# Stick-breaking attention: the order of two subtractions in a block, one from PSUM and one of a carry that comes through DRAM

## The chip, the cores and the metric

The kernel runs on one core of a Trainium2 chip. The metric is the device time of one execution in microseconds (us), median of three runs. A profile of one further execution is shown with it. In the profile PE is the matrix engine (PEld its weight load), DVE the vector engine, ACT the scalar engine, POOL GpSimd, and SP the engine that issues most DMAs. L781 is line 781 of the kernel.

## The reference, cut to what matters

One decoder block on 1024 tokens of width 1024: a state-space branch and an attention branch, merged by gates, then a feed-forward part. The change is in the attention branch, which has 8 heads of 64 and works as follows:

```
z        = (q @ k.T) / sqrt(64)                       # one head, 1024 x 1024
mask     = key_pos < query_pos
log_not  = where(mask, log_sigmoid(-z), 0)
suffix   = cumsum(log_not, over keys, reverse) - log_not
weights  = where(mask, exp(log_sigmoid(z) + suffix), 0)
out      = weights @ v
```

So the weight of a key needs the sum of log_not over all later keys up to the query. Since log_sigmoid(z) = z - softplus(z) and log_not = -softplus(z), the exponent is z minus the sum of softplus(z) over this key and all later ones.

## The kernel before, in words

Attention is worked in 40 units, one after the other. There are four pairs of heads (`hp`), each with two halves of 512 queries (`Q`). A half is swept over blocks of 128 keys (`kbs`) from the last to the first, three units for the first half (the last two key blocks share a unit) and seven for the second. So a pair of heads has ten units; I number all of them from 0 to 39, and units 10, 20 and 30 are the first ones of a pair. In every half the first three units lie on the diagonal and need the mask; they have 768, 768 and 1024 columns (two heads together), all others have 1024. Keys are on the partitions, queries on the columns.

What happens to unit i:

- `scores` (L742): PE makes z in PSUM (tile `z`, one buffer). DVE adds the mask (L763), or ACT copies (L765), into `wa`. ACT makes log(1+exp(-|z|)) in three passes (L766 to L768) into `ws`, and DVE makes softplus of it (L769). POOL rounds this to `wh` (L770) and DVE makes the remainder `wl` (L771), so that PE can multiply both parts at its faster rate without losing bits.
- `sums` (L773): PE multiplies a triangle of ones by `wh` and `wl`. The result in PSUM (tile `acc`, one buffer) holds for each key the sum over the keys of this block from it on. What the later blocks sum up to, the carry, comes in `wb` (one buffer), the same row on all 128 partitions. POOL subtracts the carry from `wa` (L781), DVE subtracts `acc` from `wa`, one head at a time (L802), and ACT takes the exponential (L803).
- In the same function the carry for the next unit is made: DVE adds the first row of `acc` to the row so far (L794 or L796, on one partition), SP stores the row into DRAM (L798, tensor `cD`), and SP loads it back on 128 partitions (L800) into `wb`.
- `values` (L805): PE multiplies the weights with V (tile `V`) and sums over the units of a half in PSUM.

The loop `attention` (L815) runs `sums` of unit i, then `values` of unit i-1, then `scores` of unit i+3 (`LOOK = 3`). In between it sets 8 matmuls of other work each time (`fillers`, L703: the projections of q and k for later heads and of a gate; their weights come by L412, are rounded by ACT L419 or POOL L421, and POOL makes the remainder in L422). PE keeps this written order (`pinned`). On DVE, ACT, POOL and SP the order within each engine is set when the program is built, by a scheduler that models when each instruction could start; at run time each engine works its list in that order, and an instruction waits for its operands with all behind it on its engine waiting too. A buffer is given to its next tile when the last reader of the old tile is done. So `acc` of unit i+1 can be written when both L802 of unit i are done, and L800 of unit i can start when L781 of unit i, the last reader of the one `wb`, is done.

The numbers of the buffers touched here are two lines of the program:

```
ZPB, MXB = 1, 2
WAB2, WSB, WHB, RWB, CBB = 5, 2, 2, 2, 1
```

Of the kernel before, what the change touches and what calls it, by code (L numbers as in the profile page):

```python
# [13 lines left out]
ALU = mybir.AluOpType  # L14
# [320 lines left out]
P = 128  # L335
# [57 lines left out]
class Block:  # L393
# [379 lines left out]
    def sums(self, u, work):  # L773


        nc, g, a, f = self.nc, u.group, u.a, u.f
        kb, fs, c = u.segs[-1]
        if g.behind is not None:
            old = slice(c.start + P if kb >= 4 * u.Q else 0, 512)
            o = slice(old.start - c.start, 512 - c.start)  # L780
            nc.gpsimd.tensor_tensor(a[:, :, o], a[:, :, o], g.behind[:, :, old], ALU.subtract)  # L781
        r = self.accp.tile([P, 2, 512], F32, name="acc")
        for x in range(2):
            for n in range(2):
                self.pinned(r[:, x, 0:f], lhsT=self.upto, rhs=u.parts[n][:, x, 0:f], start=n == 0, stop=n == 1 and g.behind is not None)
            if g.behind is None:
                for n in range(2):
                    self.pinned(r[:, x, f - P:f], lhsT=self.ones_r, rhs=u.parts[n][:, x, 0:P], start=False, stop=n == 1)
        if kb:
            past, g.row = g.row, work.tile([P, 2, 512], F32, name="row", bufs=RWB)[0:1]  # L790
            if c.start:
                nc.gpsimd.memset(g.row[:, :, 0:c.start], 0.0)
            if past is None:
                nc.vector.tensor_copy(g.row[:, :, c], r[0:1, :, fs])  # L794
            else:
                nc.vector.tensor_tensor(g.row[:, :, c], past[:, :, c], r[0:1, :, fs], ALU.add)  # L796
            d = self.cD[u.hp, u.Q, kb:kb + 1]
            nc.sync.dma_start(out=d, in_=g.row.rearrange("p a b -> p (a b)"))  # L798
            g.behind = work.tile([P, 2, 512], F32, name="wb", bufs=CBB)
            nc.sync.dma_start(out=g.behind.rearrange("p a b -> p (a b)"), in_=d[0].partition_broadcast(P))  # L800
        for x in range(2):
            nc.vector.tensor_tensor(a[:, x, 0:f], a[:, x, 0:f], r[:, x, 0:f], ALU.subtract)  # L802
        self.last_exp = nc.scalar.activation(a[:, :, 0:f], a[:, :, 0:f], AF.Exp)  # L803

    def values(self, u, out):  # L805
# [605 lines left out]
```

## Time and profile before

| | |
|---|---|
| time, median of 3 runs (lowest to highest) | 1584.97 us (1581.94 to 1589.53) |
| the profiled execution: its own time, its span | 1583.8 us, 1582.1 us |
| busy in the span: PE, DVE, ACT, POOL | 1424.0, 1094.8, 616.2, 821.3 us |
| mean granted clock of PE, as a share of full speed | 0.960 |
| attention: first matmul into `acc`, last exponential done | 420.4 us, 720.6 us from the start of the span |
| L802, DVE, out of PSUM | 80 instructions, 46.8 us busy |
| L781, POOL, the carry | 32 instructions, 67.8 us busy |

Busy is the time in which an engine had an instruction of any kind under way. A row of the profile that groups instructions gives after the bar their busy time, the mean of one, and how long the engine stood idle just before them, with what ended that wait. Idle time of an engine that nobody waits for costs nothing.

### The profile page before, as it was taken

Reading aid. Unit: us, or ns where it says so; the run is one execution under the profiler, and the core shown is the slowest. Engines: PE = TensorE matmul, PEld = TensorE weight load, DVE = VectorE, ACT = ScalarE, POOL = GpSimd, SP = SyncE. Lnnn points to the kernel's source line nnn. Section 1 sums busy time; section 2 is a strip of 40 time slices with the busy share of each in tenths; the row PEclk is TensorE's granted clock in tenths of the full one; section 3 lists DMA queues with packets and bytes.
Section 4 is the critical chain, followed back from the end, with each engine's and each line's share of the span. In section 5 each row is a group of like instructions: output and inputs, shape, how many; then the busy total and the mean of one; then the engine's idle time right before and its main releaser. Section 6 shows DMA issues by size and latency. Waiting matters only on the chain.

```text
span 1582.1 us, 18396 instructions
## 1 busy us (share of the span) xinstructions
PE 1424.0 (90%) x6578; PEld 1117.5 (71%) x6578; DVE 1094.8 (69%) x1317; ACT 616.2 (39%) x792; POOL 821.3 (52%) x642
## 2 busy tenths in 40 slices
PE   4898888799998899989799879999999998999965
PEld 2698767678755555647688668888888887787854
DVE  5548777442577787766723986666665669999978
ACT  5431111452565656565315543233323233433313
POOL 2488684010445454532420636554445468879774
PEclk9899999999999999999899989999999999999988
DMA  8456666635423233236334315333333246545302
GB/s 284 161 142 177 179 188 172 182 106 181 132 80 108 81 97 124 94 101 224 114 142 146 107 40 154 106 113 108 106 100 100 93 164 229 151 142 163 102 22 107
DMA packets 180451, 210.46 MB, mean 133 GB/s; under 512 B 28612, under 2 KB 121896, under 8 KB 180360
## 3 DMA queue, kind: packets, MB, share of 16 engines
q1 hardware_dynamic: 169288, 201.29, 40.1%
q10 hardware_dynamic: 11072, 8.00, 1.8%
q8 instruction: 52, 0.85, 0.2%
q14 instruction: 39, 0.32, 0.1%
HBM read 159.18 MB, written 48.89 MB: 132 GB/s over the span
## 4 chain that ended last, share of the span: by engine, by line
PE 30%; DVE 10%; issue 5%; POOL 4%; ACT 1%; DMA 1%; POOLq 0%; DVEq 0%; ACTq 0%
PE tq L1138 11%; PE wo L1138 9%; PE wo L1019 5%; PE gu L1138 3%; POOL pa L1191 1%; DVE f L1213 1%; POOL wb L1211 1%; POOL pb L1230 1%; DVE pb L1226 1%; DVE x L1226 1%; DVE f L1209 1%; DVE wl L1209 1%; DMA pa<-in_w_ffn_down_dram 1%; DVE ft L438 1%; PE tq L1220 0%
## 5 line engine op out<-in xcount | busy, mean ns | idle before, releaser
L438 POOL TENSOR_TENSOR ws<-wb 128x1024 f32<-128x1024 f32 x29 | 73.2, 2524 | 105.7 <-DVE wl L441 59.9
L770 POOL TENSOR_SCALAR wh<-ws 128x1024 fp32r<-128x1024 f32 (+1 forms) x40 | 38.6, 964 | 124.7 <-DVE ws L769 87.9
L422 POOL TENSOR_TENSOR wl<-ws,wh 128x1024 fp32r<-128x1024 f32 x14 | 37.1, 2656 | 116.3 <-ACT wh L419 106.9
L771 DVE TENSOR_TENSOR wl<-ws,wh 128x1024 fp32r<-128x1024 f32 (+1 forms) x40 | 66.1, 1653 | 36.8 <-POOL wh L770 36.7
L438 POOL TENSOR_TENSOR wgs<-wb 128x1024 f32<-128x1024 f32 x15 | 37.9, 2527 | 101.5 <-DVE x L441 35.1
L781 POOL TENSOR_TENSOR wa<-wa,wb 128x1024 f32<-128x1024 f32 (+2 forms) x32 | 67.8, 2120 | 31.8 <-DMA wb<-cD 26.1
L803 ACT ACTIVATE wa<-wa 128x1024 f32<-128x1024 f32 (+1 forms) x40 | 38.9, 972 | 80.3 <-DVE wa L802 75.8
L802 DVE TENSOR_TENSOR wa<-wa,acc 128x512 f32<-128x512 f32 (+1 forms) x80 | 46.8, 623 | 29.9 <-POOL wa L781 26.7
L871 DVE SCALAR_TENSOR_TENSOR acc<-aw,cond,acc 128x512 f32<-128x512 f32 x56 | 54.7, 978 | 18.1 <-DMA aw<-in_w_ada_dram 17.5
L1191 POOL TENSOR_TENSOR pa<-pa,row 128x1024 f32<-128x1024 f32 x22 | 66.3, 3034 | 1.5 <-DMA pa<-in_w_ffn_down_dram 1.5
L769 DVE SCALAR_TENSOR_TENSOR ws<-wa,ws 128x1024 f32<-128x1024 f32 (+1 forms) x40 | 53.4, 1336 | 16.4 <-ACT ws L768 16.3
L1129 POOL TENSOR_TENSOR f<-f,f 128x512 f32<-128x512 f32 x30 | 49.1, 1661 | 26.0 <-DVE f L1119 17.5
L701 PE MATMUL acc<-wh,upto 128*128 128x512 f32 (+1 forms) x80 | 32.7, 409 | 26.9 <-DVE wa L802 26.2
L766 ACT ACTIVATE ws<-wa 128x1024 f32<-128x1024 f32 (+1 forms) x40 | 38.9, 973 | 37.3 <-DVE wa L763 36.6
L419 ACT CAST wh<-ws 128x1024 fp32r<-128x1024 f32 x28 | 29.2, 1047 | 55.0 <-PE wo L1019 30.2
L1211 POOL TENSOR_TENSOR wb<-pa 128x512 f32<-128x512 f32 x23 | 40.2, 1756 | 15.7 <-DVE wxl L1209 5.5
L1118 ACT ACTIVATE f<-f 128x1024 f32<-128x1024 f32 x22 | 23.3, 1061 | 56.5 <-DVE f L1158 29.1
L701 PE MATMUL z<-q,k 64*128 64x512 f32 (+3 forms) x192 | 41.8, 526 | 3.3 <-DVE wa L763 1.7
L701 PEld LDWEIGHTS acc<-wh,upto 128*128 128x128 f32 x80 | 15.5, 194 | 37.9 <-issue 29.7
L1129 POOL TENSOR_TENSOR f<-f 128x512 f32<-128x512 f32 x20 | 42.2, 2126 | 0.0
L1220 PE MATMUL tq<-f,f 128*128 128x512 f32 x96 | 31.1, 407 | 11.8 <-DVE f L1213 11.8
L1220 PE MATMUL wo<-f,f 128*128 128x512 f32 x132 | 40.7, 389 | 0.0
(818 smaller groups left out, 4888.4 us busy)
## 6 DMA issues: line engine op xcount, KB each, us to landing
aw<-in_w_ada_dram SPq DMA_DIRECT2D x32, 512.0 KB
wb<-cD SPq DMA_DIRECT2D x32, 512.0 KB
hD<-f SPq DMA_DIRECT2D x30, 512.0 KB
ws<-in_w_in_dram SPq DMA_DIRECT2D x23, 512.0 KB
wb<-in_w_ffn_gate_dram SPq DMA_DIRECT2D x44, 256.0 KB
wb<-in_w_ffn_up_dram SPq DMA_DIRECT2D x44, 256.0 KB
pa<-in_w_ffn_down_dram SPq DMA_DIRECT2D x22, 512.0 KB
wb<-hD SPq DMA_DIRECT2D x40, 256.0 KB
```

Source lines behind the costliest of these rows:

```text
L438: (add or nc.gpsimd).tensor_tensor(st, a, b, op)
L701: return self.tc.keep_in_program_order(self.nc.tensor.matmul(*args, **kw))
L769: nc.vector.scalar_tensor_tensor(st, a, 0.0, st, ALU.max, ALU.add)
L771: nc.vector.tensor_tensor(lt, st, ht.bitcast(F32), ALU.subtract)
L781: nc.gpsimd.tensor_tensor(a[:, :, o], a[:, :, o], g.behind[:, :, old], ALU.subtract)
L871: nc.vector.scalar_tensor_tensor(acc, w[:, j], cj, acc, ALU.mult, ALU.add)
L1019: nc.tensor.matmul(ps, lhsT=mg[t // 4][k][:, a, P * (t % 4):P * (t % 4) + P], rhs=ws[k // 2][b][:, k % 2], start=(j == 0), stop=(j == 23))
L1129: nc.gpsimd.tensor_tensor(o, a, b, op)
L1138: self.nc.tensor.matmul(ps, lhsT=w[x][:, q, k], rhs=self.B[i](y, k), start=(j == 0), stop=(j == 11))
L1191: nc.gpsimd.tensor_tensor(w, w, g2, ALU.mult)
L1211: nc.gpsimd.tensor_tensor(st[:, R], u, W[p][b[0]][:, 512 * b[1]:512 * b[1] + 512], SIGN_B[i])
L1220: nc.tensor.matmul(ps, lhsT=o[x][:, P * t:P * t + P], rhs=o[y][:, R], start=(j == 0), stop=(j == 3 * np_ - 1))
```

## The change

POOL's subtraction of the carry moves from the front of `sums` to behind DVE's subtraction out of `acc`. The tile that it reads is kept in a local name, since `g.behind` is by then the tile of the next unit. Nothing else is changed; the number of instructions is the same.

```diff
         nc, g, a, f = self.nc, u.group, u.a, u.f
         kb, fs, c = u.segs[-1]
-        if g.behind is not None:
-            old = slice(c.start + P if kb >= 4 * u.Q else 0, 512)
-            o = slice(old.start - c.start, 512 - c.start)
-            nc.gpsimd.tensor_tensor(a[:, :, o], a[:, :, o], g.behind[:, :, old], ALU.subtract)
+        behind = g.behind
         r = self.accp.tile([P, 2, 512], F32, name="acc")
         for x in range(2):
             for n in range(2):
-                self.pinned(r[:, x, 0:f], lhsT=self.upto, rhs=u.parts[n][:, x, 0:f], start=n == 0, stop=n == 1 and g.behind is not None)
-            if g.behind is None:
+                self.pinned(r[:, x, 0:f], lhsT=self.upto, rhs=u.parts[n][:, x, 0:f], start=n == 0, stop=n == 1 and behind is not None)
+            if behind is None:
...
         for x in range(2):
             nc.vector.tensor_tensor(a[:, x, 0:f], a[:, x, 0:f], r[:, x, 0:f], ALU.subtract)
+        if behind is not None:
+            old = slice(c.start + P if kb >= 4 * u.Q else 0, 512)
+            o = slice(old.start - c.start, 512 - c.start)
+            nc.gpsimd.tensor_tensor(a[:, :, o], a[:, :, o], behind[:, :, old], ALU.subtract)
         self.last_exp = nc.scalar.activation(a[:, :, 0:f], a[:, :, 0:f], AF.Exp)
```

In the kernel after the change the carry's subtraction is L803 (before L781), DVE's subtraction L799 (before L802), the row L793 (before L796), its memsets L789 (before L792), the exponential L804 (before L803). The scheduler sets some neighbours anew. In the rows below a number behind a tile's name is one buffer use: `wa_4366`, `wa_4418`, `wa_4464` and `wa_4518` belong to units 16, 17, 18 and 19, and `wh_4420`, `wh_4466`, `wh_4520`, `wh_4570` and `wh_4618` to units 17 to 21.

POOL between the rounding of unit 17 and that of unit 19, before:

```order
L770 TENSOR_SCALAR wh_4420<-ws_4419 128x1024
L781 TENSOR_TENSOR wa_4366<-wa_4366,wb_4449 128x1024
L422 TENSOR_TENSOR wgl_4485<-wgs_4483,wgh_4484 128x1024
L770 TENSOR_SCALAR wh_4466<-ws_4465 128x1024
L781 TENSOR_TENSOR wa_4418<-wa_4418,wb_4503 128x1024
L770 TENSOR_SCALAR wh_4520<-ws_4519 128x1024
```

The same stretch of POOL after the change:

```order
L770 TENSOR_SCALAR wh_4420<-ws_4419 128x1024
L422 TENSOR_TENSOR wgl_4485<-wgs_4483,wgh_4484 128x1024
L803 TENSOR_TENSOR wa_4366<-wa_4366,wb_4448 128x1024
L770 TENSOR_SCALAR wh_4466<-ws_4465 128x1024
L803 TENSOR_TENSOR wa_4418<-wa_4418,wb_4502 128x1024
L770 TENSOR_SCALAR wh_4520<-ws_4519 128x1024
```

The carry of unit i stands ahead of the rounding of unit i+2 in both; the weight's remainder (L422) changed places with the carry that it followed.

DVE from the subtraction of unit 16 to that of unit 18, before:

```order
L802 TENSOR_TENSOR wa_4366<-wa_4366,acc_4495 128x512 x2
L769 SCALAR_TENSOR_TENSOR ws_4465<-wa_4464,ws_4465 128x1024
L771 TENSOR_TENSOR wl_4467<-ws_4465,wh_4466 128x1024
L796 TENSOR_TENSOR row_4546<-row_4500,acc_4541 1x1024
L802 TENSOR_TENSOR wa_4418<-wa_4418,acc_4541 128x512 x2
L769 SCALAR_TENSOR_TENSOR ws_4519<-wa_4518,ws_4519 128x1024
L763 TENSOR_TENSOR wa_4568<-z_4572,mask_3549 128x2x384
L771 TENSOR_TENSOR wl_4521<-ws_4519,wh_4520 128x1024
L796 TENSOR_TENSOR row_4598<-row_4546,acc_4593 1x1024
L769 SCALAR_TENSOR_TENSOR ws_4569<-wa_4568,ws_4569 128x2x384
L802 TENSOR_TENSOR wa_4464<-wa_4464,acc_4593 128x512 x2
```

The same stretch of DVE after the change:

```order
L799 TENSOR_TENSOR wa_4366<-wa_4366,acc_4494 128x512 x2
L769 SCALAR_TENSOR_TENSOR ws_4465<-wa_4464,ws_4465 128x1024
L771 TENSOR_TENSOR wl_4467<-ws_4465,wh_4466 128x1024
L793 TENSOR_TENSOR row_4545<-row_4499,acc_4540 1x1024
L799 TENSOR_TENSOR wa_4418<-wa_4418,acc_4540 128x512 x2
L769 SCALAR_TENSOR_TENSOR ws_4519<-wa_4518,ws_4519 128x1024
L763 TENSOR_TENSOR wa_4568<-z_4572,mask_3549 128x2x384
L771 TENSOR_TENSOR wl_4521<-ws_4519,wh_4520 128x1024
L793 TENSOR_TENSOR row_4597<-row_4545,acc_4592 1x1024
L799 TENSOR_TENSOR wa_4464<-wa_4464,acc_4592 128x512 x2
```

DVE's order stays, but for one L769 that no longer stands ahead of the subtraction of unit 18.

POOL where a weight with both its steps on POOL (L421 and L422) falls between units 19 and 21, before:

```order
L770 TENSOR_SCALAR wh_4520<-ws_4519 128x1024
L781 TENSOR_TENSOR wa_4464<-wa_4464,wb_4549 128x1024
L792 MEMSET row_4699 1x2x256
L770 TENSOR_SCALAR wh_4570<-ws_4569 128x2x384
L792 MEMSET row_4751 1x2x128
L421 TENSOR_SCALAR wh_4638<-ws_4637 128x1024
L781 TENSOR_TENSOR wa_4518<-wa_4518,wb_4601 128x1024
L422 TENSOR_TENSOR wl_4639<-ws_4637,wh_4638 128x1024
L770 TENSOR_SCALAR wh_4618<-ws_4617 128x2x384
```

The same stretch after the change:

```order
L770 TENSOR_SCALAR wh_4520<-ws_4519 128x1024
L789 MEMSET row_4699 1x2x256
L803 TENSOR_TENSOR wa_4464<-wa_4464,wb_4548 128x1024
L789 MEMSET row_4750 1x2x128
L770 TENSOR_SCALAR wh_4570<-ws_4569 128x2x384
L421 TENSOR_SCALAR wh_4638<-ws_4637 128x1024
L422 TENSOR_TENSOR wl_4639<-ws_4637,wh_4638 128x1024
L803 TENSOR_TENSOR wa_4518<-wa_4518,wb_4600 128x1024
L770 TENSOR_SCALAR wh_4618<-ws_4617 128x2x384
```

Here, too, both steps of the weight now stand ahead of the carry.

## Rows read from the trace of the kernel before

**Rows 1.** Busy us of each engine in stretches: window, length, PE, PEld, DVE, ACT, POOL, PEclk.

```profile
420.00:690.00 270.00, 249.73 (x1109) 158.62 (x1108) 200.06 (x206) 165.38 (x183) 133.48 (x97) 0.99 0.30 99
580.00:620.00 40.00, 40.00 (x181) 25.60 (x179) 29.80 (x32) 26.00 (x29) 21.84 (x16) 1.00 0.30 99
```

**Rows 2.** Who waited for whom: us in total, times, longest, whole span.

```profile
DVE wa L802 <- POOL wa L781: 26.7, 17, 4.6
...
PE acc L701 <- DVE wa L802: 26.2, 19, 5.8
POOL wa L781 <- DMA wb<-cD: 26.1, 17, 3.5
```

**Rows 3.** DVE in time: subtractions of units 0, 8, 15, 18, 35, 38.

```profile
422.26 0.99 DVE L802 TENSOR_TENSOR wa<-wa,acc 128x384 f32<-128x384 f32 x2
...
484.28 1.27 DVE L802 TENSOR_TENSOR wa<-wa,acc 128x512 f32<-128x512 f32 x2
...
537.61 1.27 DVE L802 TENSOR_TENSOR wa<-wa,acc 128x512 f32<-128x512 f32 x2
...
563.10 1.27 DVE L802 TENSOR_TENSOR wa<-wa,acc 128x512 f32<-128x512 f32 x2
...
686.42 1.28 DVE L802 TENSOR_TENSOR wa<-wa,acc 128x512 f32<-128x512 f32 x2 [1.12 <-POOL wa L781]
...
712.27 1.29 DVE L802 TENSOR_TENSOR wa<-wa,acc 128x512 f32<-128x512 f32 x2 [2.96 <-POOL wa L781]
```

**Rows 4.** DVE in time, 538 to 554 us, around units 15 to 17.

```profile
538.80 1.21 DVE L769 SCALAR_TENSOR_TENSOR ws<-wa,ws 128x1024 f32<-128x1024 f32 x1
541.28 1.22 DVE L771 TENSOR_TENSOR wl<-ws,wh 128x1024 fp32r<-128x1024 f32 x1 [1.27 <-POOL wh L770]
...
543.02 1.20 DVE L796 TENSOR_TENSOR row<-row,acc 1x1024 f32<-1x1024 f32 x1
544.96 1.28 DVE L802 TENSOR_TENSOR wa<-wa,acc 128x512 f32<-128x512 f32 x2 [0.74 <-POOL wa L781]
...
549.63 3.40 DVE L771 TENSOR_TENSOR wl<-ws,wh 128x1024 fp32r<-128x1024 f32 x1 [1.27 <-POOL wh L770]
...
554.09 1.27 DVE L802 TENSOR_TENSOR wa<-wa,acc 128x512 f32<-128x512 f32 x2
```

**Rows 5.** POOL in time: start, us, [idle before <-releaser].

```profile
528.07 1.30 POOL L781 TENSOR_TENSOR wa<-wa,wb 128x512 f32<-128x512 f32 x1 [1.88 <-DMA wb<-cD]
...
540.20 1.05 POOL L770 TENSOR_SCALAR wh<-ws 128x1024 fp32r<-128x1024 f32 x1 [4.73 <-PE acc L701]
542.55 2.38 POOL L781 TENSOR_TENSOR wa<-wa,wb 128x1024 f32<-128x1024 f32 x1 [1.30 <-DMA wb<-cD]
...
549.56 2.39 POOL L781 TENSOR_TENSOR wa<-wa,wb 128x1024 f32<-128x1024 f32 x1
...
563.36 0.83 POOL L770 TENSOR_SCALAR wh<-ws 128x768 fp32r<-128x768 f32 x1 [0.55 <-DVE ws L769]
...
568.49 2.38 POOL L422 TENSOR_TENSOR wl<-ws,wh 128x1024 fp32r<-128x1024 f32 x1
```

**Rows 6.** SP in time: the loads of the carry of units 13 and 15.

```profile
522.37 0.33 SPq L800 DMA_DIRECT2D wb<-cD  x1
...
538.98 0.34 SPq L800 DMA_DIRECT2D wb<-cD  x1
```

**Rows 7.** All engines in time, at 640 us: DVE and POOL on unit 30 and 29.

```profile
639.67 0.96 DVE L771 TENSOR_TENSOR wl<-ws,wh 128x768 fp32r<-128x768 f32 x1 [1.47 <-POOL wh L770]
639.90 2.96 POOL L781 TENSOR_TENSOR wa<-wa,wb 128x1024 f32<-128x1024 f32 x1
```

**Rows 8.** PE in time: first matmul into acc of units 20 and 26.

```profile
573.02 0.41 PE L701 MATMUL acc<-wh,upto 128*128 128x384 f32 x1 [1.40 <-DVE wa L802]
...
613.02 0.39 PE L701 MATMUL acc<-wh,upto 128*128 128x512 f32 x1
```

**Rows 9.** ACT in time: the exponential of unit 39.

```profile
719.56 1.06 ACT L803 ACTIVATE wa<-wa 128x1024 f32<-128x1024 f32 x1 [1.61 <-DVE wa L802]
```

## The prediction, made before the changed kernel was run

> **What bounds the kernel now.** I went from the page's busy shares (PE 90% of the span) to the stage that the change touches. The busy time by stretches [rows 1] shows PE busy 249.7 of 270 us from 420 to 690 us, so it stands still for 20 us there, and for some more in the tail up to 720. No more than that could come back. In the 40 us from 580 to 620 it never stands still, so nothing can be won in that part.
>
> The list of waits [rows 2] says why it stands still: 26.2 us, in 19 places, are PE waiting for DVE's subtraction (L802) to give `acc` back. DVE in turn waited 26.7 us in 17 places for POOL's carry (L781), and POOL 26.1 us for the load of the carry. Read quickly, that is one chain, and the change cuts it: `acc` no longer waits for the carry. But the two sums need not be the same events, so I looked at instructions in time.
>
> Two kinds of steps alternate. From unit 15 to unit 16 [rows 3 and 4] DVE subtracts at 537.61, works L769, waits 1.27 us for POOL's rounding, works L771 and the row, waits 0.74 us for the carry and subtracts at 544.96: 7.35 us. From unit 16 to 17 the carry was there early, POOL took it at 549.56 for 2.39 us [rows 5], and DVE's L771, begun 0.07 us later, took 3.40 instead of 1.22 us [rows 4]; the step took 9.13 us. DVE lost 2.2 us without a wait in the list. The reverse is in [rows 7]: a carry that POOL began while DVE was on L771 took 2.96 us instead of 2.38 us, and its end is that of L771 (640.63) plus 2.23.
>
> The Trainium skill ("SBUF — State Buffer", section "SBUF: two separate sides") says that GpSimd and a DVE instruction with two SBUF inputs take a shared port as an exclusive lock, and whoever begins first blocks the other for its whole length. The trace agrees with these two rows. By that rule the carry, wherever it is put, pushes L769 or L771 aside; without it the changed step below would be about 1.2 us shorter, which is my faster rival.
>
> **The change, part by part.** No instruction is added or removed. 32 carries on POOL come to stand behind the subtraction on DVE, and the exponential (ACT) behind the carry.
>
> *Removed: DVE's wait for the carry,* 26.7 us in 17 places. What is late next is DVE's own list. POOL keeps the carry of unit i ahead of the rounding of unit i+2, so the steps line up one behind the other. From one subtraction to the next in the middle of a second half: two L802, 1.20 us until the next begins; L769 1.21; the carry, released while L769 runs and held until its end, 2.38; rounding 1.05 plus 0.05; L771 1.14 until the next begins; row 1.13 [rows 4 and 5]. Sum 8.16 us. The step before the first of these has a carry of 768 columns, three quarters of 2.38, or 1.8: 7.6 us. Steps near the diagonal sum to 5 to 7 us. PE's own pace, from 573.02 to 613.02 in six steps [rows 8], is 6.67 us; these include units of 768 columns, and where most units are full I take 6.9. So PE gets `acc` earlier near the diagonal, and in the middle of each second half it waits for DVE as it does now.
>
> *Moved: the carry and its load.* The load of unit i (L800) may start only when the carry of that unit has been read, since `wb` has one buffer. Now that is one subtraction later. From issue to the carry's start was 3.57 us at unit 16, 5.70 us at unit 14, where a weight's load had been issued 0.9 us before [rows 5 and 6]. In the 8.16 us step the carry ends 4.79 us after the subtraction begins; with 0.1 us for issue the next one may begin 10.57 us after, which leaves 5.67 us for the load. So at both ends of what was seen the load just fits, and I cost it at nothing; its cover is the step itself. If it gets longer, each us is paid in full, because the rounding for unit i+2, then L771 and PE's later `acc`, stand behind the carry on POOL. Behind the load on SP's list are the next row's store, gate stores and weight loads; none is needed within a step.
>
> *Moved with it: the weights' remainder (L422),* now ahead of the carry that it followed. 11 of them fall into attention, 2.38 us each [rows 5]. Beside DVE's row and L802 (2.3 us a step) they are hidden; where L421 stands in front, they are not. From unit 18 to 20, in order: L802 1.20, L769 0.91, carry 2.38, rounding 0.83, L421 1.05 (as a rounding of that size), L771 0.91, L422 2.38, L769 0.91, carry 2.38, rounding 0.83, L771 0.91, row 0.60 = 15.3 us, against 13.3 for two steps at PE's pace. (Units of 768 columns at three quarters; the row of 512 at half of 1.20.) A bound below is zero, all hidden; above, 11 times 2.38 = 26.2 us. I take those places where the list shows a chain, about 7 us in all.
>
> *Moved: the exponential.* It ends about 6 us after the subtraction instead of 2.4. PE wants its values one unit later, a step of 7 to 8 us; PE may be held for a us, which it makes up before the next `acc`. Behind it ACT has three more passes (L766 to L768) of about the exponential's length of 1.06 us [rows 9], and these end about 0.2 us before DVE wants them; where ACT also rounds a weight in between, about a us, DVE waits up to 0.8 us, in four places.
>
> *The sum.* I followed the 40 units with these durations, at each step taking the later of DVE's list and PE's pace, and compare with the subtractions in [rows 3].
> - Units 0 to 8: 60.5 us, before 62.0: -1.5. Most of it at unit 5, where DVE waited for a late load.
> - 8 to 15: 47.8, before 53.3: -5.5. Seven steps, mostly near the diagonal, at PE's 6.7 each are 46.9; before, late carries held DVE at units 9, 11, 12 and 14 (the last is in [rows 5]).
> - 15 to 18: 24.4 (7.6 + 2 x 8.16, and 0.5 for ACT), before 25.5: -1.1.
> - 18 to 35: 128.1, before 123.3: +4.8. Before, PE ran through most of this without waiting. Now 17 steps at 6.9 are 117.3, plus 2.0 at unit 20 (above), 2.2 at unit 24 (the mask addition stands behind L771 behind the carry behind L422, and PE waits for `z`), 4.3 for units 25 to 28 (two steps of 8.16, one of 7.6, a weight), about 2.3 for a mask that comes late at unit 33 and weights before it.
> - 35 to 38: 22.8, before 25.9: -3.1. No wait for the carry.
> - 38 to the end of the last exponential: 12.1, before 8.4 (720.62 less 712.27 [rows 3 and 9]): +3.7. The end is now a chain of carries: 2.5 until POOL may begin the carry of unit 38, 2.4, load 3.65, the last carry 2.4, exponential 1.1.
>
> Together -2.7 us. Behind 720 us PE has work at hand, so the end of attention moves the rest with it. The profiled execution was 1583.8 us, so 1581.1; the median of the runs is 1.2 us above that, so 1582.3.
>
> **The rivals.**
> - *Faster: PE gets `acc` when it wants it.* If the carry slips into DVE's waits for POOL or beside the instructions with a PSUM input, L769 is not in its chain, and a step is 8.16 - 1.2 = 6.95 us, PE's pace. For the 12 long steps (7.97 on average) that is 12.2 us more, and 1570 us; with the places of L422 hidden too, 1563. For it: 26.2 us of PE's waits have just the released buffer as their end. Against it: L771 at 3.40 us, and POOL's order.
> - *Slower: the load with one buffer sets the pace.* Place: 20 carries in the second halves with their load behind the carry before. It decides from 5.67 us from issue to start on, and each us above costs a us a unit: at 6.7 us, 20 us, less the 2.7 won: 1602 us. For it: 5.70 at unit 14 with a weight's 512 KB ahead, and weights now stand directly ahead of more of these loads. Against it: a weight's load needs no carry, so it is issued some us before; in most units 3.6 is what was seen.
> - *Slower: the weights' remainders.* If all 11 stay in the chain (26.2 instead of the 7 counted): 19 us more, 1601 us; half of them, 1592.
>
> **How the numbers follow.** Within 0.5% (7.9 us, about what a measurement of this kernel can tell from no change) is 1577 to 1593. My forecast, waits that trade places, has 0.55 and its own range is 1576 to 1590. The faster rival has 0.25, the load 0.09, the remainders 0.11. Of the forecast a small part lies below 1577, of the remainders' rival a third lies within the bound. That makes 0.28 faster, 0.55 the same, 0.17 slower. The range leaves out a tenth on either side: 1566 to 1597.
>
> **What would show it.** Right: no wait of DVE's L799 (the subtraction) for POOL; PE's wait for `acc` no longer 26 but still 15 to 25 us; L769 or POOL's carry longer by what the other holds; steps of about 8.2 us between full units; at the end two loads in the chain of the last exponential. The forecast is wrong if PE's waits for `acc` fall under 10 us (faster), if POOL's waits for the load grow above 26 us and the rounding stands behind them (the load), or if the units with L421 and L422 take over 10 us a step (remainders).

## The result and the profile after

The changed kernel takes 1577.7 us (median of 11 runs, 1571.1 to 1580.2), the kernel before 1586.8 us beside it. The ratio is 0.9949, 95% interval [0.9935, 0.9963]: 0.5% faster. The forecast was 1582 in a range of 1566 to 1597; the ratio lies at the edge of the 0.5% that the forecast counted as the same. The profiled execution took 1579.3 us, its span 1577.6.

The waits of the changed kernel from 420 to 725 us (us in total, times, longest) answer to [rows 2]:

```profile
ACT wa L804 <- POOL wa L803: 81.3, 31, 5.4
DVE wl L771 <- POOL wh L770: 67.6, 39, 3.3
POOL wa L803 <- DVE wa L799: 49.3, 17, 3.8
...
PE mm L701 <- ACT wa L804: 20.4, 15, 5.3
...
POOL wa L803 <- DMA wb<-cD: 17.3, 6, 4.1
...
PE acc L701 <- DVE wa L799: 7.4, 6, 2.5
```

DVE's 26.7 us of waiting for the carry are gone: L799 never waits for POOL. PE's wait for `acc` fell from 26.2 to 7.4 us, but PE now waits 20.4 us for the exponential, which it did for 0.4 us before. And DVE waits 67.6 us for POOL's rounding, 36.7 before. Waits traded places. The busy time agrees (columns as in [rows 1]):

```profile
420.00:690.00 270.00, 252.80 (x1145) 163.22 (x1142) 195.10 (x214) 169.77 (x190) 148.70 (x98) 1.00 0.31 99
580.00:620.00 40.00, 37.80 (x166) 24.21 (x164) 25.84 (x28) 25.10 (x28) 25.34 (x16) 1.00 0.30 100
```

PE gained only 3 us of work in the first window, and in the second, where it never stood still before, it now does for 2.2 us. The column to look at is POOL's: 148.7 us busy, before 133.5, with one instruction more in the window. Two groups of lines show where these us come from (before, whole span; busy us, mean ns | idle before):

```profile
L781 POOL TENSOR_TENSOR wa<-wa,wb 128x1024 f32<-128x1024 f32 (+2 forms) x32 | 67.8, 2120 | 31.8 <-DMA wb<-cD 26.1 <-ACT ws L768 2.3 <-ACT ws L767 1.6
L771 DVE TENSOR_TENSOR wl<-ws,wh 128x1024 fp32r<-128x1024 f32 (+1 forms) x40 | 66.1, 1653 | 36.8 <-POOL wh L770 36.7
```

The same two after the change:

```profile
L803 POOL TENSOR_TENSOR wa<-wa,wb 128x1024 f32<-128x1024 f32 (+2 forms) x32 | 81.1, 2534 | 72.9 <-DVE wa L799 49.3 <-DMA wb<-cD 17.3 <-ACT gst L738 2.9
...
L771 DVE TENSOR_TENSOR wl<-ws,wh 128x1024 fp32r<-128x1024 f32 (+1 forms) x40 | 52.7, 1317 | 67.7 <-POOL wh L770 67.6
```

The 32 carries take 13.3 us longer, the 40 remainders L771 13.4 us less; L769 takes 53.4 us in both kernels. What DVE and POOL hold each other for was handed from one to the other, not taken away. One step between full units, DVE and POOL in time, answers to [rows 4 and 5]:

```profile
541.11 1.27 DVE L799 TENSOR_TENSOR wa<-wa,acc 128x512 f32<-128x512 f32 x2
542.31 1.21 DVE L769 SCALAR_TENSOR_TENSOR ws<-wa,ws 128x1024 f32<-128x1024 f32 x1
542.46 3.31 POOL L803 TENSOR_TENSOR wa<-wa,wb 128x1024 f32<-128x1024 f32 x1 [3.48 <-DVE wa L799]
...
545.74 1.04 POOL L770 TENSOR_SCALAR wh<-ws 128x1024 fp32r<-128x1024 f32 x1
545.81 1.06 ACT L804 ACTIVATE wa<-wa 128x1024 f32<-128x1024 f32 x1 [5.43 <-POOL wa L803]
546.82 1.22 DVE L771 TENSOR_TENSOR wl<-ws,wh 128x1024 fp32r<-128x1024 f32 x1 [3.30 <-POOL wh L770]
...
546.92 1.08 PE L701 MATMUL mm<-wa,V 128*64 128x512 f32 x4 [1.43 <-ACT wa L804]
547.96 1.20 DVE L793 TENSOR_TENSOR row<-row,acc 1x1024 f32<-1x1024 f32 x1
549.09 1.26 DVE L799 TENSOR_TENSOR wa<-wa,acc 128x512 f32<-128x512 f32 x2
```

POOL's carry begins 0.15 us after L769 and ends at 545.77, 2.25 us after L769: 3.31 us instead of 2.38. Then the rounding, L771, the row, the next subtraction: 7.98 us, link by link as forecast. PE waits 1.43 us there for an exponential that stands behind the carry.

In what follows a step goes from one unit's subtraction (L799, or its line in another kernel) to that of the next, a full step lies between units of 1024 columns, and the tail is the last interval of the table below. Attention by intervals, from the starts of the subtractions (us; the last column is experiment e5 below, where PE hardly waits):

| units | forecast | before | after | e5 |
|---|---|---|---|---|
| 0 to 8 | 60.5 | 62.0 | 58.8 | 52.7 |
| 8 to 15 | 47.8 | 53.3 | 47.1 | 46.7 |
| 15 to 18 | 24.4 | 25.5 | 26.1 | 20.1 |
| 18 to 35 | 128.1 | 123.3 | 122.3 | 113.5 |
| 35 to 38 | 22.8 | 25.9 | 20.5 | 18.2 |
| 38 to the last exponential's end | 12.1 | 8.4 | 14.6 | 8.2 |
| sum | 295.7 | 298.4 | 289.4 | 259.4 |

So attention is 9.0 us shorter, the time by the medians 9.1. That the two agree so well is in part luck: the two profiled executions differ by 4.5 us only, since in the second the first subtraction came 2.9 us later (425.2 us) and from the end of attention to the end of the span it is 861.5 us before and 863.0 after. In the runs below, but for e8, the first subtraction comes between 419.5 and 425.5 us, so a difference of times and one of attention can part by some us.

### The profile page after: what moved, and what is told of

Same layout as the page of the kernel before. It is cut to its first block, busy times and chain, and to the rows that moved or that the text cites. A ratio compares the mean times of both kernels' runs of the same rounds, so it can differ in the third digit from the quotient of the medians.

```text
span 1577.6 us, 18363 instructions
## 1 busy us (share of the span) xinstructions
PE 1418.9 (90%) x6578; PEld 1115.5 (71%) x6578; DVE 1078.4 (68%) x1317; ACT 613.0 (39%) x792; POOL 836.7 (53%) x642
## 4 chain that ended last, share of the span: by engine, by line
PE 29%; DVE 10%; issue 5%; POOL 4%; ACT 1%; DMA 1%; DVEq 0%; POOLq 0%; ACTq 0%
PE tq L1139 12%; PE wo L1139 9%; PE wo L1020 5%; PE gu L1139 3%; POOL pa L1192 1%; DVE f L1214 1%; POOL pb L1231 1%; DVE x L1227 1%; DVE pb L1227 1%; POOL wb L1212 1%; DVE f L1210 1%; DVE wl L1210 1%; DMA pa<-in_w_ffn_down_dram 1%; DVE ft L438 1%; POOL ws L1212 0%
## 5 line engine op out<-in xcount | busy, mean ns | idle before, releaser
L803 POOL TENSOR_TENSOR wa<-wa,wb 128x1024 f32<-128x1024 f32 (+2 forms) x32 | 81.1, 2534 | 72.9 <-DVE wa L799 49.3
L422 POOL TENSOR_TENSOR wl<-ws,wh 128x1024 fp32r<-128x1024 f32 x14 | 39.6, 2834 | 119.5 <-ACT wh L419 70.4
L771 DVE TENSOR_TENSOR wl<-ws,wh 128x1024 fp32r<-128x1024 f32 (+1 forms) x40 | 52.7, 1317 | 67.7 <-POOL wh L770 67.6
L804 ACT ACTIVATE wa<-wa 128x1024 f32<-128x1024 f32 (+1 forms) x40 | 38.9, 971 | 82.4 <-POOL wa L803 81.3
L769 DVE SCALAR_TENSOR_TENSOR ws<-wa,ws 128x1024 f32<-128x1024 f32 (+1 forms) x40 | 53.4, 1334 | 13.1 <-ACT ws L768 12.6
L701 PE MATMUL mm<-wa,V 128*64 128x512 f32 (+3 forms) x192 | 40.7, 517 | 20.5 <-ACT wa L804 20.4
L419 ACT CAST wh<-ws 128x1024 fp32r<-128x1024 f32 x28 | 29.2, 1048 | 57.3 <-PE wo L1020 32.2
L799 DVE TENSOR_TENSOR wa<-wa,acc 128x512 f32<-128x512 f32 (+1 forms) x80 | 46.6, 616 | 1.2 <-PE acc L701 1.2
L1221 PE MATMUL tq<-f,f 128*128 128x512 f32 x96 | 31.1, 407 | 11.8 <-DVE f L1214 11.8
L768 ACT ACTIVATE ws<-ws 128x1024 f32<-128x1024 f32 (+1 forms) x40 | 38.9, 973 | 1.1
```

The lines of the kernel that those rows point to most:

```text
L701: return self.tc.keep_in_program_order(self.nc.tensor.matmul(*args, **kw))
L769: nc.vector.scalar_tensor_tensor(st, a, 0.0, st, ALU.max, ALU.add)
L771: nc.vector.tensor_tensor(lt, st, ht.bitcast(F32), ALU.subtract)
L803: nc.gpsimd.tensor_tensor(a[:, :, o], a[:, :, o], behind[:, :, old], ALU.subtract)
L1221: nc.tensor.matmul(ps, lhsT=o[x][:, P * t:P * t + P], rhs=o[y][:, R], start=(j == 0), stop=(j == 3 * np_ - 1))
```

## The experiments

Ratios are against the kernel before, run on the same chip beside each. "Attention" is from the first subtraction to the end of the last exponential in the profiled execution.

| kernel | time, us | ratio [95%] | attention, us |
|---|---|---|---|
| changed | 1577.7 | 0.9949 [0.9935, 0.9963] | 289.4 |
| e1 row in place | 1572.0 | 0.9945 [0.9923, 0.9967] | 287.5 |
| e2 two carry buffers | 1566.4 | 0.9905 [0.9882, 0.9927] | 282.4 |
| e3 values two behind | 1571.5 | 0.9940 [0.9916, 0.9963] | 291.2 |
| e4 all carries late | 1568.2 | 0.9911 [0.9886, 0.9937] | 285.1 |
| e5 changed, short carry | 1540.3 | 0.9732 [0.9712, 0.9752] | 259.4 |
| e6 before, short carry | 1543.9 | 0.9761 [0.9743, 0.9779] | 260.3 |
| e7 some carries late | 1569.2 | 0.9922 [0.9902, 0.9942] | 287.9 |
| e8 the same, two buffers | 1590.7 | 1.0045 [1.0031, 1.0059] | 276.6 |
| e9 carry on DVE | 1553.5 | 0.9802 [0.9776, 0.9829] | 264.7 |
| e10 on DVE, two buffers | 1544.4 | 0.9746 [0.9721, 0.9771] | 261.8 |
| e11 before, two buffers | 1584.5 | 1.0005 [0.9985, 1.0025] | 301.3 |
| e12 before, on DVE, two buffers | 1577.9 | 0.9964 [0.9945, 0.9984] | 294.9 |

### Is it the buffer of the load? (e1, e2, e11)

A second `wb` needs room, which the row makes by staying in one tile (e1, the control):

```diff
-            past, g.row = g.row, work.tile([P, 2, 512], F32, name="row", bufs=RWB)[0:1]
-            if c.start:
+            past = g.row
+            if past is None:
+                g.row = work.tile([P, 2, 512], F32, name="row", bufs=1)[0:1]
...
```

> The changed kernel with the carry's row summed in place in one buffer instead of two (frees 4 KB per partition; 8 of 16 small memsets on POOL fall away). It is the base for the next three. My theory (the DVE and POOL list of a full unit, 8.0 us, sets the pace) expects no change: 1574 to 1582 us. The rival that the carry's way through DRAM sets the pace expects no change either, unless the store now holds the next row: then up to 10 us slower.

The ratio is that of the changed kernel; the time is lower, as is that of the kernel before beside it (1580.3 us). e2 adds the buffer:

```diff
-WAB2, WSB, WHB, RWB, CBB = 5, 2, 2, 2, 1
+WAB2, WSB, WHB, RWB, CBB = 5, 2, 2, 2, 2
```

> As e1, with two buffers for the carry that is loaded, so that a load need not wait for the carry before to be read. My theory: the steps between full units stay at 8.0 us, POOL's wait for the load (17.3 us in 6 places) falls under 6 us, and at the end of attention the two last loads start early, 4 to 5 us; in all 4 to 8 us less than e1, 1567 to 1574. Rival (the load with one buffer sets the pace): steps of full units fall to 7 us and the time by 15 to 20 us, 1558 to 1563.

It gained 5.7 us on e1. POOL's waits for the load fell from 17.1 us to 6.3, and full steps stayed at 7.97 to 8.07 us. Attention is 5.1 us shorter than in e1, 3.1 of them in the tail (11.5 us instead of 14.6). The carry waits for its load in the tail and at a few units; the load does not set the step. The same edit in the order before (e11):

> The kernel before the change with two buffers for the loaded carry, the row kept in place. Theory A (before, a load stands behind the carry in the one buffer: 2.4 us for the carry and 3.6 to 5.7 for the load make 6.1 to 8.2 us a step, and DVE's subtraction waits for that): DVE's waits for POOL fall from 26.7 to under 15 us, 8 to 12 us less, 0.993 of the time before. Theory B (the load begins when the row is stored, not when the buffer is free, and the rest is DVE and POOL holding each other): waits as before, 0.999.

Theory B held: the time is that of the kernel before (the profile is of its slowest execution, 1589.7 us). POOL still waited 28.3 us for the load (26.1 with one buffer) and DVE 34.7 us for POOL. In the order before, the load waits for the row's store (at unit 15 the one was issued at 540.76, the other at 542.00), and a free buffer is of no use.

### Is it PE's wait for the exponential? (e3)

`values` of a unit is written one unit later in the loop:

```diff
-            if i > 0:
-                u = units[i - 1]
+            if i > 1:
+                u = units[i - 2]
```

> As e1, with the product with V two units behind the sums instead of one (six buffers of wa), so that PE has a unit more before it wants an exponential. My theory: PE's wait for exponentials (20.4 us in 15 places) vanishes from the list, but turns into a wait for acc, since DVE and POOL set the pace; steps of full units stay at 8.0 us, time within 3 us of e1. Rival (PE's wait for the exponential is the new bound): 12 to 20 us less than e1, 1558 to 1566.

PE's waits for the exponential fell from 20.4 to 5.2 us, those for `acc` rose from 7.4 to 18.8, full steps stayed at 7.99 and 8.08 us and the time did not move. PE waits for the same chain, at whichever of the two places comes first in its list.

### Does it help to take the carry out of the chain? (e4, e7, e8)

The carry is made to follow L771 of two units on, for all units (e4) or only for key blocks 4 to 2 of a second half (e7); e8 is e7 with two buffers:

```diff
+            carry = nc.gpsimd.tensor_tensor(a[:, :, o], a[:, :, o], behind[:, :, old], ALU.subtract)
+            n = self.units.index(u) + 2
+            if u.Q and kb in (4, 3, 2):
+                self.tc.add_manual_dep(carry.ins, self.units[n].wl.ins.name, ..., reason="lag")
```

> As e3, and the carry of unit i waits until the remainder wl of unit i+2 is made, so that POOL rounds before it subtracts the carry and the carry lies beside DVE's row and the two subtractions out of PSUM. My theory (POOL's carry stands in the chain between L769 and the rounding, and the port keeps it from L769 and L771): steps of full units fall from 8.0 to PE's 6.9 us, 12 to 16 us less than e3, 1558 to 1568. Rival (the exponential or the load is the bound): no gain, or slower, since the carry comes later and the load behind it too.

> The kernel with values two units behind and the row in place, and the carry held until the next unit's L771 only in the three units of a second half whose key blocks are 4, 3 and 2 (12 of 32 carries); elsewhere the order of the changed kernel. Theory (a step of 8 us falls to PE's pace when the carry is not ahead of the rounding; that the earlier run with all carries late gained only 3 us came from the late loads near the diagonal): full steps about 6.9 us in these places without long steps elsewhere, 10 to 13 us less than the kernel with values two behind: 0.986 of the time before. Rival (the time saved in one step is lost in the next, since the load of the next carry begins later): no better than all carries late, 0.991.

> The same with two buffers for the loaded carry (room for it made by one buffer less for a staged gate and the triangle inside the mask's tile). Theory: the load may begin before the carry is read, so a late carry delays no load; full steps at PE's pace and a tail some 3 us shorter, 4 to 6 us less than the kernel with the late carries in second halves: 0.982 of the time before. Rival (the two edits win the same time): as the one with two buffers alone, 0.990.

The full steps did fall: in e4 to 6.55, 7.32 and 6.06 us from unit 15 on (10.05, 7.98 and 8.08 after the change). But I expected 12 to 16 us in e4 and about as much in e7; they gave 3.3 and 2 to 3 us. In e7 the steps from 15 to 18 sum to 20.8 us instead of 26.1, and those from 18 to 35 to 123.3 instead of 122.3; POOL's waits for the load rose from 21.8 us (e3) to 31.1. The rival was right: a later carry frees the one buffer later, and the next unit pays. The tail pays most: 18.4 us in e7 and 18.5 in e4, 13.3 in e3. With two buffers those waits are 7.9 us, and attention is 11 us shorter than in e7, where theory gave 4 to 6. e8's time is no measure of this: to make room I took a buffer from the tile `gst` of an earlier stage and laid the triangle inside the mask's tile. Up to the start of attention DVE then waited 57.3 us for `gst` to be stored (15.9 in e7), and the first subtraction came at 449.7 instead of 420.6 us.

### Is it the carry's length? (e5, e6)

In both orders the carry is subtracted from the first 16 columns of each head only, and the rest of it is left out; loads and waits stay:

```diff
+            o, old = slice(o.start, o.start + 16), slice(old.start, old.start + 16)
```

> The changed kernel with the carry subtracted from the first 16 columns of each head only; the rest of the carry is left out, all loads, stores and waits stay. Theory (the chain from subtraction to subtraction in the second halves is L769, carry, rounding, L771, row, and its length is set by the carry's 2.4 us between L769 and the rounding): full steps fall from 8.0 to about 6.9 us, PE's pace, in some 12 places, and the tail loses two carries of 2.4 us: 13 + 4.5 = 17 us less than the changed kernel, about 0.984 of the time before. Rival (the load sets the pace, the carry's length hardly matters): full steps stay at 7.5 to 8, POOL's waits for the load take the carry's place; only the tail gains, 0.992 of the time before.

> The kernel before the change with the same short carry (16 columns of each head), the rest left out. Theory (before, DVE's subtraction waited for the load of the carry, whatever the carry's length, and the change's gain is that DVE no longer waits for it): DVE still waits some 15 us or more for POOL, in the units near the diagonal, but the steps that were long by the lock (L771 of 3.4 us) fall; gain 5 to 10 us, 0.995 of the time before. Rival (what DVE lost was the carry's length and the lock, and not the load): DVE's waits for POOL nearly vanish, gain 15 to 20 us as in the changed kernel with the same short carry, 0.988.

Both fell further than I expected, to within 3.5 us of each other: e5 by the ratios some 34 us below the changed kernel, twice the 17 expected, and e6 39 us below the kernel before, where theory gave 5 to 10 and the rival 15 to 20. For e6 the rival holds in the time, though not in its sign: POOL waits 44.5 us for loads (26.1 before) and DVE still 16.2 us for POOL, and that costs at most the 3.5 us to e5. So in both orders the cost was the carry's length on POOL, and not the load. The runs don't part its own 2.4 us from the time that POOL and DVE hold each other. What DVE's part of that holding comes to shows in L769 and L771, whose work is the same in all: together they take 119.5 us before, 106.1 after and 92.8 in e5. One step in e5, DVE and POOL in time:

```profile
519.06 1.27 DVE L799 TENSOR_TENSOR wa<-wa,acc 128x512 f32<-128x512 f32 x2
...
520.26 1.21 DVE L769 SCALAR_TENSOR_TENSOR ws<-wa,ws 128x1024 f32<-128x1024 f32 x1
520.47 1.11 POOL L804 TENSOR_TENSOR wa<-wa,wb 128x32 f32<-128x32 f32 x1 [4.37 <-DVE wa L799]
...
521.65 1.05 POOL L770 TENSOR_SCALAR wh<-ws 128x1024 fp32r<-128x1024 f32 x1
522.74 1.23 DVE L771 TENSOR_TENSOR wl<-ws,wh 128x1024 fp32r<-128x1024 f32 x1 [1.27 <-POOL wh L770]
...
525.67 1.27 DVE L799 TENSOR_TENSOR wa<-wa,acc 128x512 f32<-128x512 f32 x2
...
527.02 0.25 POOL L804 TENSOR_TENSOR wa<-wa,wb 128x32 f32<-128x32 f32 x1
```

A carry of 32 columns is still held to the end of L769 (1.11 us; the next one, with nothing under way on DVE, took 0.25), but now that costs POOL nothing: the rounding needs L769 as well. The step is 6.61 us, and PE's wait for `acc` is 0.7 us in the whole of attention: this is PE's pace.

### The full carry on DVE (e9, e10, e12)

```diff
-            nc.gpsimd.tensor_tensor(a[:, :, o], a[:, :, o], behind[:, :, old], ALU.subtract)
+            nc.vector.tensor_tensor(a[:, :, o], a[:, :, o], behind[:, :, old], ALU.subtract)
```

> The changed kernel with the full carry subtracted by DVE instead of POOL, nothing left out. After the short carry (which took both orders 40 us down) the theory is that the carry's 2.4 us on POOL, between L769 and the rounding, and the time that it and DVE hold each other, are what is lost. On DVE it should take about the 1.2 us of L769 or L771, in the gap in which DVE waits 1.27 us for the rounding: DVE's list is then 1.20 + 1.21 + 1.21 + 1.14 + 1.13 = 5.9 us a full step, near PE's pace of 6.7 with what is left of that gap. Full steps about 7.0 instead of 8.0; 15 to 25 us less than the changed kernel, 0.982 of the time before. Rival (DVE now waits for the carry's load itself, with the row and L771 behind it, as it did before the change): DVE waits 20 us or more for the load, 0.995 or above.

> The same with two buffers for the loaded carry, the row kept in place. Theory: a load may begin before the carry is read, so DVE waits for a load less, and the tail has one load less in its chain; 4 to 6 us less than the carry on DVE with one buffer, 0.979 of the time before. Rival (with the carry in DVE's gap the load is in time in any case): no difference beyond 2 us.

Both as the theory had it in direction and about in size. From e9 to e10 the time fell by 9 us where 4 to 6 were expected, but attention by 2.9 us only; the rest lies ahead of it (the first subtraction came 4.0 us earlier) and behind it (1.9 us), and I can't put it down to the second buffer. e10 is the fastest full kernel here, 2.5% below the kernel before. DVE and POOL in time in e10, from unit 16 to 17:

```profile
528.02 1.27 DVE L801 TENSOR_TENSOR wa<-wa,acc 128x512 f32<-128x512 f32 x2
...
529.32 1.23 DVE L805 TENSOR_TENSOR wa<-wa,wb 128x1024 f32<-128x1024 f32 x1
...
530.46 1.22 DVE L769 SCALAR_TENSOR_TENSOR ws<-wa,ws 128x1024 f32<-128x1024 f32 x1
531.87 1.05 POOL L770 TENSOR_SCALAR wh<-ws 128x1024 fp32r<-128x1024 f32 x1 [3.00 <-DVE ws L769]
532.95 1.22 DVE L771 TENSOR_TENSOR wl<-ws,wh 128x1024 fp32r<-128x1024 f32 x1 [1.27 <-POOL wh L770]
534.09 1.20 DVE L795 TENSOR_TENSOR row<-row,acc 1x1024 f32<-1x1024 f32 x1
535.23 1.27 DVE L801 TENSOR_TENSOR wa<-wa,acc 128x512 f32<-128x512 f32 x2
```

The carry takes 1.23 us on DVE here against 2.4 to 4.4 on POOL after the change, and the step 7.21 instead of 7.98. DVE is busier (227.2 of 270 us, 195.1 after the change), and it stays below PE. PE from 420 us to the end of attention, first in the kernel before, then in e10:

```profile
420.00:720.00 300.00, 271.07 (x1177) 171.13 (x1175) 218.32 (x224) 177.47 (x195) 145.36 (x103) 0.97 0.30 98
```

```profile
420.00:683.00 263.00, 259.91 (x1173) 168.53 (x1171) 223.23 (x256) 177.10 (x195) 88.53 (x63) 0.99 0.33 112
```

Nearly the same number of matmuls in 37 us less. PE's idle time fell from 28.9 to 3.1 us, and its busy time by 11 us, at a granted clock of 0.99 instead of 0.97. So the bound that I read from PE's idle time at the start of the prediction ("no more than that could come back") was too low. Part of the 11 us is the clock: it was 0.94 before from 540 to 570 and from 630 to 660 us, 0.95 from 690 to 705 and 0.71 from 705 to 720, and in e10 1.00 up to 660 us and 0.93 behind. Busy time multiplied by what was missing of full clock gives 7.3 us before and 1.4 in e10, an estimate of some 6 of the 11. The rest, ends that the trace only models among it, is not settled.

In e10 PE sets the pace nearly to the end. Its first matmuls into `acc` of units 10 and 20:

```profile
485.39 0.33 PE L701 MATMUL acc<-wh,upto 128*128 128x384 f32 x1
...
552.17 0.33 PE L701 MATMUL acc<-wh,upto 128*128 128x384 f32 x1
```

These ten steps of PE take 66.8 us, as they do in e5, and each of them is the same in both runs to 0.02 us; they take 79.1 us before and 73.2 after the change. The five steps from unit 21 to 26, in which PE never stood still before, take 33.0 us in all three, before, e5 and e10: there, as the prediction said, nothing was to be won.

The last run asks what the order is worth with the carry on DVE, by moving it back in front (the same edits on the kernel before):

> The kernel before the change with the carry on DVE and two carry buffers, the row kept in place: as the best kernel so far, but with the carry's subtraction ahead of the sums out of PSUM. It tells what the order is worth once POOL's long carry is gone. Theory (the carry's length on POOL was the cost in both orders, and the order decides little): as with the short carry, where the two orders stood 3.5 us apart; 3 to 6 us above the same kernel with the changed order, 0.978 of the time before. Rival (with the carry on DVE its wait for the load stops the subtraction and all behind it, so the order is worth what DVE waited before, 20 us or more): 0.988 or above.

My theory fell. The rival was right in direction and size: 33 us above e10 in time and in attention, a ratio of 0.9964 against 0.9746, which differs from the kernel before by less than half a per cent. DVE in time and POOL beside it, in e12:

```profile
538.69 1.23 DVE L771 TENSOR_TENSOR wl<-ws,wh 128x1024 fp32r<-128x1024 f32 x1 [1.28 <-POOL wh L770]
539.30 2.85 POOL L422 TENSOR_TENSOR wgl<-wgs,wgh 128x1024 fp32r<-128x1024 f32 x1 [0.65 <-ACT wgh L419]
...
540.43 2.80 DVE L781 TENSOR_TENSOR wa<-wa,wb 128x1024 f32<-128x1024 f32 x1
...
543.16 1.20 DVE L798 TENSOR_TENSOR row<-row,acc 1x1024 f32<-1x1024 f32 x1
544.29 1.26 DVE L804 TENSOR_TENSOR wa<-wa,acc 128x512 f32<-128x512 f32 x2
```

Its waits (us, times, longest):

```profile
PE acc L701 <- DVE wa L804: 28.8, 17, 4.1
...
DVE wa L781 <- DMA wb<-cD: 16.8, 18, 2.8
```

In front, the carry delays the row, the subtraction and `acc`, by its load (16.8 us, 2.0 in e10) and by what POOL holds it for, as L422 does here: its 32 instructions take 48.5 us, 33.4 in e10. These two differences are 30 us together, near the 33 in the time. That they are the cause is argued from this sum; no run shortens the load or clears POOL in this order. Behind the subtraction the load has more time, and `acc` is free first.

## Why the prediction came out as it did

**The chain was right.** No wait of L799 for POOL; the step of 8.16 us measured 7.98 to 8.08, with the carry held to the end of L769. The gain lies where it was forecast, before unit 15 (-9.5 us, forecast -7.0) and from 35 to 38 (-5.4, forecast -3.1), and so does the loss in the tail (+6.3, forecast +3.7). The Trainium skill ("SBUF — State Buffer", section "SBUF: two separate sides") says that whoever begins first blocks the other for its whole length; the runs agree, with 3.31 us for a carry of 2.38 behind L769, and 3.40 for an L771 of 1.22 behind L422.

**The mis-sized term is "18 to 35: 128.1, +4.8".** It measured 122.3, -1.0, and that is nearly the whole miss (-9.0 instead of -2.7). The base of 17 steps at 6.9 us was too long: with PE hardly waiting, e5 takes 113.5 us, 6.68 a step, not 117.3. That is 3.8 of the 5.8 us; the stalls on top were 8.8 us where I had 10.8: 1.8 to unit 20 (2.0 forecast), 1.5 from 20 to 25 (2.2), 3.5 from 25 to 28 (4.3), 2.0 from 28 to 35 (2.3). The intervals fit, two of the reasons do not. PE's steps, from the first matmul into `acc` of one unit to that of the next, are those of e5 from unit 21 to 25 and from 30 to 35, so nothing was lost to a late mask addition at units 24 and 33. PE lost time from 18 to 21 and from 25 to 30, with 8.58 and 8.15 us from 28 to 30 (6.61 and 6.83 in e5).

**Remainders (L422): right at units 18 to 20, missed at unit 15.** 18 to 20 took 14.9 us, forecast 15.3. At unit 15 I had none in the chain; there L422 began 0.07 us before L771, which took 3.40 us, and the step 10.05. So 15 to 18 came out 1.7 us over.

```profile
536.59 2.39 POOL L422 TENSOR_TENSOR wgl<-wgs,wgh 128x1024 fp32r<-128x1024 f32 x1
536.66 3.40 DVE L771 TENSOR_TENSOR wl<-ws,wh 128x1024 fp32r<-128x1024 f32 x1 [0.67 <-POOL wh L770]
```

**Load: "the load just fits".** Nearly: POOL's waits for it fell from 26.1 to 17.3 us, and the rival of the load did not come. But a second buffer (e2) took 5.1 us off attention, 3.1 in the tail, where the forecast counts a load, and 2.0 elsewhere, where I had put it at nothing.

**The tail.** Two loads stand in its chain, as forecast. It took 14.6 us instead of 12.1, since POOL could begin the carry of unit 38 only 4.7 us after the subtraction, where I had 2.5: the carry before it was held for 4.38 us by L422 on DVE and by L769, and its load came that much later. The interval before it was 2.3 us shorter than forecast, so the two together fit.

**The exponential: "held for a us, which it makes up".** PE waited 20.4 us for it in 15 places, far more; but e3 shows that this is not the bound.

**The signs.** "Acc waits of 15 to 25 us" failed: 7.4. By my list that spoke for the faster rival. It was a bad sign: in PE's list the values stand ahead of the next `acc`, so the same lateness showed as a wait for the exponential; with the values a unit later (e3) it is 18.8 us of `acc` waits. By the letter the sign for the remainders (over 10 us a step) came true as well, with 11.39 us from unit 19 to 20 and 10.05 from 15 to 16. The first comes from how a step is counted: DVE subtracted the two heads of unit 19 apart, at 560.70 and 564.37, and PE's steps there were 7.94 and 8.00 us. The second is the L422 above.

**The faster rival** did not come, but what it speaks of was worth more than I gave it. I gave 12 to 19 us to L769 leaving the chain. Without the long carry on POOL attention is 30 us shorter (e5), 25 with the full carry on DVE (e9) and 28 with two buffers besides (e10).

**What no run parts.** With the two lines the scheduler also moved L422 and one L769. No run moves the carry and leaves these neighbours where they were, so how much of the 9 us is theirs is not shown.

## What to carry to other kernels

When an edit removes a wait, sum the busy time of each group before and after as well as the waits: here 13 us left DVE's rows and appeared in POOL's, without a wait in any list. Ask of an instruction not only where it stands but on which engine: with two carry buffers the new order is worth 1.0% with the carry on POOL (e2 against e11) and 2.2% with it on DVE (e10 against e12). And a wait for a load tells nothing of its price until the load or the waiter is made short.

## What was not expected of the hardware

- POOL and DVE hold each other even when one of them has little to do: a 32-column subtraction took 1.11 us behind L769 and 0.25 us with DVE at rest.
- POOL's rounding, which reads one tensor, is held too: in e10 it took 1.61 us from 523.50, behind a carry that DVE began at 523.25 (0.94 us), and 1.05 us alone. DVE's instructions that read PSUM were not: beside a POOL L422 from 526.45 to 528.86 the row took 1.20 and L801 1.27 us.
- The same subtraction of 128 x 1024 is 1.23 us on DVE and 2.38 us on POOL.
